# A list-scheduled fp32 encoder layer: GpSimd operations that wait for their planned VectorE predecessor on the shared SBUF path, and a planner that lets transfers land later

## The chip, the cores and the metric

One core of one Trainium2 chip. The metric is device microseconds (us) of one execution. Engine names are those of the profile: PE (TensorE matmul), PEld (its weight loads), DVE (VectorE), ACT (ScalarE), POOL (GpSimd), SP (the queue that issues every DMA here).

## The reference, cut to what matters

Two inputs, a prompt of 512 tokens and a sample of 1024, go through one encoder layer of width 1024, with the same weights:

```python
x = layer_norm(x, ln_in_g, ln_in_b)
h = x @ w_in                                   # 2048 columns: conv value, conv gate, rnn x, rnn gate
c = c_val * sigmoid(c_gate)
c = silu(layer_norm(depthwise_conv(c, width 31)))
for each of 2 directions:                      # forward, backward
    xd = depthwise_conv(r_x, width 4)
    r, i = sigmoid(xd @ w_a + b_a), sigmoid(xd @ w_x + b_x)     # 8 heads of 64
    a = exp(-8 * r * softplus(-lam)); b = sqrt(-expm1(2 log a)) * (i * xd)
    hd = linear recurrence h[t] = a[t] * h[t-1] + b[t]
rec = (hf + hb) * gelu(r_gate)
x = layer_norm(alpha * x + concat(c, rec) @ w_out)
u = depthwise_conv(x @ w_up, width 3)          # 2 x 2816 columns: val, gate
x = layer_norm(alpha * x + (gelu(gate) * val) @ w_down)
```

## The kernel before, in words

Everything is fp32. A matmul is three products of parts: every operand is split into a high part (rounded to fp32r by an ACTIVATE) and a low part (the rest, by one subtraction on DVE or POOL), and PE adds hi·hi, hi·lo and lo·hi. So each weight that is loaded has to be split by ACT, and then by DVE or POOL, before PE can use it (`split`, `weight`; some weights' low parts are written to DRAM, `lo_up_d` and `lo_down_d`, and loaded again by the later blocks).

The work comes in this order. Head: the layer norm of the input pages (128 tokens by 1024), transposes, and h of the sample and the prompt (`w_in`). Then the prompt's mixer (convolutions, gates, decay, scan), its output projection and its feed-forward part (FFN, `ffn(None)`); the sample in two blocks of 512 tokens, block 1 first: `mixer_s(1)` runs beside the prompt's FFN, `mixer_s(0)` beside `ffn(1)`, and `ffn(0)`, the last 530 us, has no mixer beside it. The FFN goes through 22 pairs of 128 columns (`up(p)`): two up projections, three taps of a convolution on ACT and DVE, gelu on ACT, one product of 128x512 on "any" of DVE and POOL (on POOL in the prompt's FFN), a split, and after some pairs the down projection, whose sums DVE adds to y. The tail is the last four pages' layer norm (`ln2`), which for two of the pages has its two 128x1024 operations (times g, plus b) on POOL, and the stores to `out_s`.

Nothing is issued in the order of this text. Each helper (`tt` L197, `stt` L206, `ts` L220, `act` L236, `dma` L247, `mm` L258, `transposes` L266) records an operation with its cost in ns, a priority, and its predecessors. `Sched.emit` (L270) then plays the list through: at each step it takes, over the five engines, the operation that could start earliest (of those ready within LOOK = 160 ns the one of the best priority), for "any" operations on the engine that would end sooner, and notes the order. The five engines' instruction streams are written out in that order, and nothing moves later. LAT holds the planned delay between engines (155 ns from DVE to POOL).

One SBUF path is modelled as shared: `takes_port` says that a POOL operation that reads SBUF, and a DVE operation with two SBUF inputs, use it one at a time, and `port` is the time from which it is free. This is in the plan alone; on the chip the two streams run as they come. A transfer's end is planned in `emit` as `bus = max(bus, t + 1500) + nbytes / 360`, so 2.96 us after its issue for 512 KB when no other is on the bus.

POOL's work is the power of -0.5 in every layer norm (128x1), the low parts of the gate inputs (128x512, `chain`: `lo_eng="pool"`), the decay product of each chain (128x512, `rg_decay(..., "pool")`), the products of the prompt's FFN, and what "any" sends there.

Of the kernel before, what the change touches and what calls it, by code (L numbers as in the profile page):

```python
# [44 lines left out]
class View:  # L45


    def __init__(self, buf, idx, post=()):
        self.buf, self.idx, self.post = buf, idx, post
        sel = buf.index[idx]  # L50
        self.n = int(sel.size)
        self.mask = buf.mask(sel)
# [73 lines left out]


class Op:
    __slots__ = ("i", "eng", "cost", "fn", "prio", "preds", "succs", "np", "rt", "end", "tab", "nbytes", "start", "both", "shared")


LAT = {("act", "dve"): 142, ("act", "pe"): 227, ("act", "pool"): 170, ("act", "act"): 143,
       ("dve", "act"): 150, ("dve", "pe"): 233, ("dve", "pool"): 155, ("dve", "dve"): 127,
       ("pe", "act"): 197, ("pe", "dve"): 196, ("pe", "pe"): 3, ("pool", "dve"): 60, ("pool", "act"): 75,
       ("pool", "pe"): 150, ("pool", "pool"): 102}
LOOK = 160
ACT_TABLE = {AF.Sigmoid: "s", AF.Tanh: "sge", AF.Gelu_apprx_tanh: "g", AF.Sqrt: "q", AF.Silu: "u", AF.Exp: "e"}


class Sched:  # L140
    def __init__(self, nc, sbuf_pool, psum_pool):
        self.nc, self.sbuf_pool, self.psum_pool = nc, sbuf_pool, psum_pool
        self.slots = {}
        self.ops = []
        self.nbuf = 0
        self.first = {}
# [77 lines left out]
    def act(self, out, a, func, scale=1.0, bias=0.0, prio=None):  # L224
        ptr = [s for s in (scale, bias) if isinstance(s, View)]
        cost = out.n / 1.2 + (51 if a.psum else 93) + 90 * len(ptr)
        f = lambda s: s() if isinstance(s, View) else s
        kw = {}
        if isinstance(scale, View) or scale != 1.0:
            kw["scale"] = None  # L230
        if isinstance(bias, View):
            kw["bias"] = None

        def emit():
            k = {n: f({"scale": scale, "bias": bias}[n]) for n in kw}
            self.nc.scalar.activation(out=out(), in_=a(), func=func, **k)  # L236
        return self.op("act", cost, emit, [a] + ptr, [out], prio, tab=ACT_TABLE.get(func))

# [13 lines left out]
    def mm(self, out, pairs, start, stop, prio=None, w=None):  # L252

        cost = len(pairs) * ((out.n / 512) * 213 + 14)

        def emit():
            for i, (a, b) in enumerate(pairs):
                self.nc.tensor.matmul(out=out(), lhsT=a(), rhs=b(), start=start and i == 0,  # L258
                                      stop=stop and i == len(pairs) - 1)
        r = [v for p in pairs for v in p]  # L260
        return self.op("pe", cost, emit, r, [out], prio)

    def transposes(self, outs_ins, whole, ident, prio=None):
        def emit():
            for o, i in outs_ins:
                self.nc.tensor.transpose(o(), i(), ident())  # L266
        return self.op("pe", 116 * len(outs_ins), emit, [i for _, i in outs_ins] + [ident], [whole], prio)


    def emit(self):  # L270
        ops = self.ops
        for o in ops:
            o.succs, o.np, o.rt, o.start = [], len(o.preds), {}, None
        for o in ops:
            for p in o.preds:
                ops[p].succs.append(o)
        engines = ("sp", "pe", "act", "dve", "pool")
        free = dict.fromkeys(engines, 0.0)
        ready = {e: [] for e in engines}
        table = "i"  # L280
        bus = 0.0

        def choices(o):
            return ("dve", "pool") if o.eng == "any" else (o.eng,)

        port = 0.0

        def takes_port(o, e):
            return e == "pool" and o.shared >= 1 or e == "dve" and o.shared >= 2

        def ready_on(o, e):
            rt = o.rt.get(e, 0.0)
            return max(rt, port) if takes_port(o, e) else rt

        def cost_on(o, e):
            return o.cost[e] if isinstance(o.cost, dict) else o.cost

        def enable(o):
            for e in choices(o):
                ready[e].append(o)  # L300
        for o in ops:
            if o.np == 0:
                enable(o)
        order = []
        while len(order) < len(ops):
            best = None
            for e in engines:
                lst = ready[e]
                if not lst:
                    continue  # L310
                t = max(free[e], min(ready_on(o, e) for o in lst))
                if best is not None and t >= best[0]:
                    continue
                pick = None
                for o in lst:
                    rt = ready_on(o, e)
                    if rt > t + LOOK:
                        continue
                    if o.eng == "any":
                        f = "pool" if e == "dve" else "dve"  # L320
                        if max(free[f], ready_on(o, f)) + o.cost[f] < max(t, rt) + o.cost[e]:
                            continue
                    key = (o.prio + (TABLE_PEN if o.tab and table not in o.tab else 0.0), o.i)
                    if pick is None or key < pick[0]:
                        pick = (key, o, max(t, rt))
                if pick is not None and (best is None or pick[2] < best[0]):
                    best = (pick[2], e, pick[1])
            t, e, o = best
            for f in choices(o):
                ready[f].remove(o)  # L330
            cost = cost_on(o, e)
            if e == "act" and o.tab and table not in o.tab:
                cost += 1283
                table = o.tab[0]
            o.eng, o.cost, o.start = e, cost, t
            free[e] = t + cost
            if takes_port(o, e):
                port = t + cost
            if e == "sp":
                bus = max(bus, t + 1500) + o.nbytes / 360.0  # L340
                o.end = bus
            else:
                o.end = t + cost
            for s in o.succs:
                for f in choices(s):
                    s.rt[f] = max(s.rt.get(f, 0.0), o.end + LAT.get((e, f), 100))
                s.np -= 1
                if s.np == 0:
                    enable(s)
            order.append(o)  # L350
        self.place()
        self.order = order
        self.makespan = max(o.end for o in ops)
        for o in order:
            if o.both:
                o.fn(o.eng)
            else:
                o.fn()


TABLE_PEN = 3.0
# [2 lines left out]
def body(ctx, tc, xp, xs, w_in, gw, w_out, w_up, w_down, par, gb, out_p, out_s):  # L364
    nc = tc.nc
    sb = ctx.enter_context(tc.tile_pool(name="sb", bufs=1))
    ps = ctx.enter_context(tc.tile_pool(name="ps", bufs=1, space=PSUM))
    S = Sched(nc, sb, ps)
    f32, f32r = F32, F32R

    x0_d = [tc.dram_tile([NP_TOK // 128, 128, D], F32, name="x0p_d"),
# [7 lines left out]

    P = S.buf("par", [NPAR])  # L380
    idn = S.buf("idn", [128])
    cst = S.buf("cst", [8])
    S.load(P.all, par, prio=1.5)

    def mk_ident():
        make_identity(nc, idn.ap())
    S.op("pool", 1500, mk_ident, [], [idn.all], prio=-1)
    S.op("pool", 100, lambda: nc.gpsimd.memset(cst[0:1](), -0.5), [], [cst[0:1]], prio=-2)
    S.op("pool", 100, lambda: nc.gpsimd.memset(cst[1:2](), 0.5), [], [cst[1:2]], prio=-2)
# [722 lines left out]
```

## Time and profile before

| what | value |
|---|---|
| time, median of 3 runs (lowest, highest) | 1616.22 us (1615.35, 1616.29) |
| the profiled execution's own time | 1616.81 us |
| its span in the profile | 1615.0 us |
| granted TensorE clock, mean of that execution | 0.993 |
| PE busy | 1556.7 us (96%), 7012 instructions |
| DVE busy | 1200.4 us (74%), 1867 instructions |
| ACT busy | 820.3 us (51%), 1019 instructions |
| POOL busy | 188.1 us (12%), 159 instructions |
| DMA queue of SP | 314.9 MB, 58.8% of 16 engines |

The span is what the profiler sees from the first to the last instruction; the execution's own time is 1.8 us more, and 0.6 us above the median of the runs. Busy time counts an instruction from its start to its end, so an instruction that is held back by something inside its run counts as busy. An engine's idle time is listed with what ended it.

### The profile page before, as it was taken

To read this page: it belongs to the slowest core of one execution; us is meant where nothing else is said; L and a number is where in the kernel's file an instruction comes from. 1 tells how busy PE (TensorE), PEld (TensorE's weight loads), DVE (VectorE), ACT (ScalarE), POOL (GpSimd) and SP (SyncE) were. 2 spreads that over 40 slices of the span, in tenths; PEclk is the share of its full clock that TensorE was granted. 3 is DMA by queue.
4 is the path that set the end of the run, shared out by engine and by line. 5 is a ranking of instruction groups with operands and counts; after the bars stand their busy time and mean duration, and the time that the engine had idled before them with its cause. 6 is when DMAs were issued, how large, how long until landed. Compare 5 with 4: busy or idle time off the path is not lost.

```text
span 1615.0 us, 19015 instructions
## 1 busy us (share of the span) xinstructions
PE 1556.7 (96%) x7012; PEld 1281.2 (79%) x7012; DVE 1200.4 (74%) x1867; ACT 820.3 (51%) x1019; POOL 188.1 (12%) x159
## 2 busy tenths in 40 slices
PE   5999999999999999999999999999999999999996
PEld 5887888887778777788888878788887888888784
DVE  8999995498989999873689899844438644545448
ACT  3737775148687974344359833352424433333341
POOL 3102121002122222010101100000001000000003
PEclk9999999999999999999999999999999999999998
DMA  9862335466567455657686676476665556555541
GB/s 359 299 219 96 126 118 187 165 208 206 158 193 223 153 189 190 202 169 248 204 259 201 214 251 202 160 253 200 195 212 196 195 194 195 202 183 195 184 162 65
DMA packets 107517, 316.09 MB, mean 196 GB/s; under 512 B 11936, under 2 KB 12064, under 8 KB 107296
## 3 DMA queue, kind: packets, MB, share of 16 engines
q1 hardware_dynamic: 107424, 314.88, 58.8%
q8 instruction: 55, 0.90, 0.2%
q14 instruction: 38, 0.31, 0.1%
HBM read 247.72 MB, written 67.11 MB: 195 GB/s over the span
## 4 chain that ended last, share of the span: by engine, by line
PE 50%; DVE 26%; ACT 10%; DMA 9%; issue 4%; SPq 0%; POOL 0%; DVEq 0%; ACTq 0%; POOLq 0%
PE b L258 48%; DVE b L206 15%; DVE b L197 9%; ACT b L236 7%; DMA b<-w_up 6%; ACT L236 3%; PE b L266 1%; DMA b<-mixs_d 1%; DMA b<-w_down 1%; DVE b L708 1%; DMA lo_in_d<-b 1%; DVE b L413 0%; DMA b<-lo_out_d 0%; DMA b<-xp 0%; SPq L247 0%
## 5 line engine op out<-in xcount | busy, mean ns | idle before, releaser
L258 PE MATMUL b<-b,b 128*128 128x512 f32 (+1 forms) x6724 | 1532.1, 389 | 24.5 <-DVE b L197 15.9
L258 PEld LDWEIGHTS b<-b,b 128*128 128x128 f32 x6724 | 1247.8, 189 | 293.6 <-DVE b L197 26.5
L206 DVE SCALAR_TENSOR_TENSOR b<-b,b,b 128x511 f32<-128x511 f32 (+12 forms) x848 | 593.0, 715 | 177.5 <-ACT b L236 156.6
L236 ACT ACTIVATE b<-b 128x1024 fp32r<-128x1024 f32 (+4 forms) x576 | 447.3, 799 | 533.6 <-PE b L258 197.2
L197 DVE TENSOR_TENSOR b<-b,b 128x512 f32<-128x512 f32 (+6 forms) x483 | 396.0, 840 | 122.8 <-ACT b L236 70.4
L236 ACT ACTIVATE b<-b,b 128x512 f32<-128x512 f32 (+1 forms) x337 | 256.9, 784 | 220.9 <-PE b L258 160.3
L197 POOL TENSOR_TENSOR b<-b,b 128x1 f32<-128x1 f32 (+3 forms) x89 | 113.6, 1282 | 674.1 <-DVE b L220 443.7
L236 ACT ACT_TABLE_LOAD x106 | 136.0, 1283 | 26.7 <-DVE b L206 23.9
L197 POOL TENSOR_TENSOR b<-b 128x512 f32<-128x512 f32 x52 | 73.3, 1409 | 609.1 <-ACT b L236 597.6
L206 DVE SCALAR_TENSOR_TENSOR b<-b,b 128x512 f32<-128x512 f32 (+2 forms) x81 | 53.6, 673 | 62.5 <-PE b L258 61.8
L413 DVE BATCH_NORM_STATS2 b<-b 128x6 f32<-128x512 f32 x84 | 56.7, 688 | 12.1 <-PE b L266 6.7
L197 DVE TENSOR_TENSOR b<-b 128x512 f32<-128x512 f32 (+3 forms) x80 | 46.5, 600 | 25.8 <-ACT b L236 24.9
L206 DVE SCALAR_TENSOR_TENSOR b<-b 128x512 f32<-128x512 f32 (+1 forms) x110 | 56.0, 518 | 6.8 <-POOL b L197 3.4
L266 PE MATMUL b<-b,b 128*128 128x128 f32 x288 | 40.0, 281 | 17.9 <-DVE b L206 12.1
L266 PEld LDWEIGHTS b<-b,b 128*128 128x128 f32 x288 | 34.8, 145 | 23.9 <-DVE b L206 10.7
L708 DVE TENSOR_TENSOR_SCAN b<-b 128x512 f32<-128x512 f32 x24 | 29.3, 1223 | 0.7
L1046 POOL MEMSET b<- 128x128 f32 x1 | 0.2, 207 | 134.6 <-PE b L258 134.6
L220 DVE TENSOR_SCALAR b<-b 128x1 f32<-128x1 f32 (+1 forms) x61 | 10.3, 171 | 1.7
L415 DVE BATCH_NORM_AGGREGATE b<-b 128x2 f32<-128x12 f32 (+1 forms) x48 | 9.5, 199 | 0.9
L243 DVE COPY b<-b 128x2 f32<-128x2 f32 x44 | 6.6, 150 | 0.0
L220 DVE TENSOR_SCALAR b<-b,b 128x512 f32<-128x512 f32 x2 | 0.9, 484 | 0.0
L900 POOL MEMSET b<- 128x1 f32 x8 | 0.3, 99 | 1.0 <-PE b L258 1.0
(11 smaller groups left out, 1.6 us busy)
## 6 DMA issues: line engine op xcount, KB each, us to landing
b<-w_up SPq DMA_DIRECT2D x132, 512.0 KB, 4.4
b<-lo_up_d SPq DMA_DIRECT2D x88, 512.0 KB, 4.2
b<-w_down SPq DMA_DIRECT2D x132, 256.0 KB, 4.0
lo_up_d<-b SPq DMA_DIRECT2D x44, 512.0 KB, 5.1
b<-lo_down_d SPq DMA_DIRECT2D x88, 256.0 KB, 3.5
b<-w_in SPq DMA_DIRECT2D x32, 512.0 KB, 5.2
b<-w_out SPq DMA_DIRECT2D x24, 512.0 KB, 4.4
lo_down_d<-b SPq DMA_DIRECT2D x44, 256.0 KB, 5.3
```

Of the source, the lines that this page charges most:

```text
L197: return self.op(eng, cost if eng == "any" else cost[eng], lambda e=eng: self.engine(e).tensor_tensor(out=out(), in0=a(), in1=b(), op=op), ...
L206: o = self.op("dve", cost, lambda: self.nc.vector.scalar_tensor_tensor(out=out(), in0=a(), scalar=s() if isinstance(s, View) else s, in1=b ...
L220: return self.op(eng, cost, lambda: e.tensor_scalar(out=out(), in0=a(), scalar1=f(s1), scalar2=f(s2), op0=op0, **({"op1": op1} if op1 is n ...
L236: self.nc.scalar.activation(out=out(), in_=a(), func=func, **k)
L243: return self.op("dve", cost, lambda: self.nc.vector.tensor_copy(out(), a()), [a], [out], prio)
L258: self.nc.tensor.matmul(out=out(), lhsT=a(), rhs=b(), start=start and i == 0, stop=stop and i == len(pairs) - 1)
L266: self.nc.tensor.transpose(o(), i(), ident())
L413: S.op("dve", c.n * 1.0417 + 69, lambda i=i, c=c: nc.vector.bn_stats(out=sm_[6 * i:6 * i + 6](), in_=c()), [c], [sm_[6 * i:6 * i + 6]], prio)
L415: S.op("dve", 211, lambda: nc.vector.bn_aggr(out=sm_[12:14](), in_=sm_[0:6 * n]().rearrange("p (a b) -> p a b", a=n)), [sm_[0:6 * n]], [sm ...
L708: S.op("dve", out.n * 2.0833 + 69, lambda: nc.vector.tensor_tensor_scan(out=out(), data0=a(), data1=b(), initial=0.0, op0=ALU.mult, op1=AL ...
L900: S.op("pool", 100, lambda z=z: nc.gpsimd.memset(z.f32(), 0.0), [], [z], ev)
L1046: S.op("pool", 200, lambda: nc.gpsimd.memset(E0.all.f32(), 0.0), [], [E0.all], 60)
```

## The change

A POOL operation that takes the shared path right after a DVE operation is planned LAT[dve, pool] = 155 ns later than the path is free, and the DVE operation, `holder`, is remembered. When the streams are written, the POOL instruction gets a dependency on that DVE instruction, so that on the chip it waits on DVE's semaphore. No DVE instruction is made to wait for POOL. Apart from that every transfer, load or store, is planned to end LAND = 1400 ns later; its wait on the chip is unchanged. Both numbers move the order of all five engines. Helpers' lines grow by 3 (`tt` is L200 after the change).

```diff
+LAND = 1400.0
...
-        port = 0.0
+        port, holder = 0.0, None
...
         def ready_on(o, e):
             rt = o.rt.get(e, 0.0)
-            return max(rt, port) if takes_port(o, e) else rt
+            if not takes_port(o, e):
+                return rt
+            return max(rt, port + (LAT["dve", "pool"] if e == "pool" and holder is not None else 0.0))
...
             if takes_port(o, e):
                 port = t + cost
+                if e == "pool":
+                    o.after = holder
+                holder = o if e == "dve" else None
             if e == "sp":
                 bus = max(bus, t + 1500) + o.nbytes / 360.0
-                o.end = bus
+                o.end = bus + LAND
...
         for o in order:
-            if o.both:
-                o.fn(o.eng)
-            else:
-                o.fn()
+            o.ins = o.fn(o.eng) if o.both else o.fn()
+            if o.after is not None:
+
+                self.tc.add_manual_dep(o.ins.ins, o.after.ins.ins.name, mybir.DependencyInfo(
+                    mybir.DependencyClass.Sync, mybir.DependencyReason.DATA), reason="port")
```

(`Sched` is given `tc` for this, and `Op` has two more slots.)

Where the order moves, at the three places that the prediction speaks of. In the rows b9, b16 are pages of the sample's input, b26 to b36 weights of `w_in` with their parts, b10 to b20 the layer norms' small values.

The head on POOL, before:

```order
L197 TENSOR_TENSOR b13_106<-b13_106,b3_116 128x1 [waits DVE_49]
L197 TENSOR_TENSOR b27_82<-b26_97,b27_82 128x1024 [waits DMAHW4_49,Activation_49]
L197 TENSOR_TENSOR b30_83<-b29_98,b30_83 128x1024 [waits DMAHW6_49,Activation_49]
L197 TENSOR_TENSOR b17_107<-b17_107,b3_116 128x1 [waits DVE_49]
L197 TENSOR_TENSOR b33_84<-b32_99,b33_84 128x1024 [waits DMAHW0_49,Activation_49]
L197 TENSOR_TENSOR b20_108<-b20_108,b3_116 128x1 [waits DVE_49]
L197 TENSOR_TENSOR b83_109<-b83_109,b3_116 128x1 [waits DVE_49]
L197 TENSOR_TENSOR b36_85<-b35_175,b36_85 128x1024 [waits DMAHW7_49,Activation_49]
```

and now:

```order
L200 TENSOR_TENSOR b13_106<-b13_106,b3_116 128x1 [waits DVE_49]
L200 TENSOR_TENSOR b27_82<-b26_97,b27_82 128x1024 [waits DMAHW4_49,Activation_49]
L200 TENSOR_TENSOR b17_107<-b17_107,b3_116 128x1 [waits DVE_49]
L200 TENSOR_TENSOR b30_83<-b29_98,b30_83 128x1024 [waits DMAHW6_49,Activation_49]
L200 TENSOR_TENSOR b20_108<-b20_108,b3_116 128x1 [waits DVE_49]
L200 TENSOR_TENSOR b33_84<-b32_99,b33_84 128x1024 [waits DMAHW0_49,Activation_49]
L200 TENSOR_TENSOR b83_109<-b83_109,b3_116 128x1 [waits DVE_49]
L200 TENSOR_TENSOR b36_85<-b35_176,b36_85 128x1024 [waits DMAHW7_49,DVE_49,Activation_49]
```

The second weight split (b30) now stands behind the power of the third page's norm (b17), whose DVE wait now names a DVE instruction behind the second STT of page 1.

The mixer of block 1 beside the prompt's FFN, on POOL (b283 is the low part of a gate input, b280 to b282 the chains' values, b324 the FFN's products), before:

```order
L197 TENSOR_TENSOR b283_2882<-b281_2885,b283_2882 128x512 [waits PE_49,Activation_49,Pool_49]
L197 TENSOR_TENSOR b283_2882<-b282_2904,b283_2882 128x512 [waits PE_49,Activation_49]
L197 TENSOR_TENSOR b280_2855<-b280_2855 128x512 [waits Activation_49]
L197 TENSOR_TENSOR b324_2914<-b324_2914 128x512 [waits Activation_49]
L197 TENSOR_TENSOR b281_2885<-b281_2885 128x512 [waits Activation_49]
```

and now:

```order
L200 TENSOR_TENSOR b283_2881<-b281_2884,b283_2881 128x512 [waits PE_49,DVE_49,Activation_49,Pool_49]
L200 TENSOR_TENSOR b283_2881<-b282_2903,b283_2881 128x512 [waits DVE_49,PE_49,Activation_49]
L200 TENSOR_TENSOR b280_2855<-b280_2855 128x512 [waits Activation_49]
L200 TENSOR_TENSOR b324_2913<-b324_2913 128x512 [waits DVE_49,Activation_49]
L200 TENSOR_TENSOR b281_2884<-b281_2884 128x512 [waits DVE_49,Activation_49]
```

The operations are the same, and four of these five now also wait for DVE. Of POOL's operations other than the powers 10 named DVE among their waits before, and 55 do now.

The tail on DVE (b686, b687 and b460 are the last pages, b739 holds g and b, b902 the last page's small values), before:

```order
L197 TENSOR_TENSOR b687_7119<-b687_7119,b893_11629 128x512 [waits PE_49]
L197 TENSOR_TENSOR b686_8111<-b686_8111,b739_7884 128x1024 [waits Activation_49]
L413 BN_STATS b902_11643<-b687_7119 128x6 [waits DVE_49]
L415 BN_AGGR b902_11643<-b902_11643 128x2 [waits DVE_49]
L220 TENSOR_SCALAR b902_11643<-b902_11643 128x1 [waits DVE_49]
L197 TENSOR_TENSOR b686_8111<-b686_8111,b739_7884 128x1024
L197 TENSOR_TENSOR b687_7119<-b687_7119,b739_7884 128x1024 [waits Activation_49]
L197 TENSOR_TENSOR b687_7119<-b687_7119,b739_7884 128x1024 [waits DVE_49]
L206 SCALAR_TENSOR_TENSOR b687_7119<-b687_7119,b902_11643,b739_7884 128x1024
L206 SCALAR_TENSOR_TENSOR b687_7119<-b687_7119,b902_11643,b739_7884 128x1024 [waits DVE_49,Pool_49]
```

and now:

```order
L200 TENSOR_TENSOR b687_7035<-b687_7035,b893_11629 128x512 [waits PE_49]
L200 TENSOR_TENSOR b686_8111<-b686_8111,b739_7864 128x1024 [waits Activation_49]
L200 TENSOR_TENSOR b686_8111<-b686_8111,b739_7864 128x1024 [waits DVE_49]
L200 TENSOR_TENSOR b687_7035<-b687_7035,b739_7864 128x1024 [waits Activation_49]
L200 TENSOR_TENSOR b687_7035<-b687_7035,b739_7864 128x1024 [waits DVE_49]
L422 BN_STATS b902_11643<-b687_7035 128x6
L424 BN_AGGR b902_11643<-b902_11643 128x2 [waits DVE_49]
L223 TENSOR_SCALAR b902_11643<-b902_11643 128x1 [waits DVE_49]
L209 SCALAR_TENSOR_TENSOR b687_7035<-b687_7035,b902_11643,b739_7864 128x1024
L209 SCALAR_TENSOR_TENSOR b687_7035<-b687_7035,b902_11643,b739_7864 128x1024 [waits Pool_49]
```

The last page's statistics now come behind the four 128x1024 operations of the two pages before it. On POOL the first operation on b460 now waits for the last of these four (before: for ACT alone), and the last power (b902) waits for the first of the two SCALAR_TENSOR_TENSOR (before: for the TENSOR_SCALAR).

Engine choices move too: the 128x512 product of the last FFN is on POOL once (six times before), two more low parts and one norm operation of 128x1024 go to DVE, and two 128x1024 and one 128x511 go to POOL. ACT loads its tables 98 times (106 before). Matmuls and DMAs are the same in number.

## Rows read from the trace of the kernel before

**Rows 1.** Busy time by stage: head, prompt's mixer, two mixer stages, last FFN.

```profile
core 0: us, PE busy (x) PEld busy (x) DVE busy (x) ACT busy (x) POOL busy (x), PEclk, DMA share, GB/s
0.00:50.00 50.00, 32.50 (x239) 31.17 (x240) 43.24 (x64) 21.07 (x26) 16.46 (x20) 1.00 0.95 352
50.00:330.00 280.00, 277.99 (x1271) 229.66 (x1270) 233.69 (x355) 162.61 (x204) 38.20 (x30) 1.00 0.50 170
330.00:750.00 420.00, 405.36 (x1770) 328.69 (x1769) 371.84 (x499) 275.76 (x339) 76.20 (x53) 0.99 0.60 193
750.00:1060.00 310.00, 306.03 (x1370) 252.17 (x1369) 260.41 (x421) 158.75 (x191) 26.46 (x30) 1.00 0.65 215
1060.00:1590.00 530.00, 525.69 (x2331) 432.31 (x2330) 272.08 (x500) 197.35 (x256) 17.03 (x18) 1.00 0.57 189
```

**Rows 2.** Waits of PE, 0 to 50 us: total us, times, longest.

```profile
PE b L266 <- DVE b L206: 11.6, 2, 10.7
PE b L266 <- DVE b L415: 5.7, 1, 5.7
```

**Rows 3.** Timeline of the head, DVE and PE: start, length, idle before.

```profile
15.15 3.13 DVE L206 SCALAR_TENSOR_TENSOR b<-b,b,b 128x1024 f32<-128x1024 f32 x1
25.72 2.75 DVE L206 SCALAR_TENSOR_TENSOR b<-b,b,b 128x1024 f32<-128x1024 f32 x1
18.43 1.94 PE L266 MATMUL b<-b,b 128*128 128x128 f32 x8 [5.75 <-DVE b L415]
```

**Rows 4.** Waits of PE, 330 to 750 us.

```profile
PE b L258 <- DVE b L197: 8.1, 10, 3.4
PE b L258 <- POOL b L197: 1.4, 1, 1.4
```

**Rows 5.** Timeline, PE behind its waits at 450 and 602 us.

```profile
449.92 5.36 PE L258 MATMUL b<-b,b 128*128 128x512 f32 x16 [1.37 <-POOL b L197]
601.88 6.44 PE L258 MATMUL b<-b,b 128*128 128x512 f32 x20 [3.42 <-DVE b L197]
```

**Rows 6.** Busy time of the stretch behind the first, and of a quiet one.

```profile
449.90:453.30 3.40, 3.38 (x9) 2.67 (x9) 3.26 (x7) 3.34 (x5) 1.22 (x1) 0.54 0.69 248
1070.00:1200.00 130.00, 130.00 (x576) 107.69 (x575) 47.73 (x80) 44.97 (x54) 0.31 (x2) 1.00 0.63 206
```

**Rows 7.** Groups by form, POOL then ACT: busy us, mean ns | idle before.

```profile
L197 POOL TENSOR_TENSOR b<-b,b 128x512 fp32r<-128x512 f32 x24 | 36.2, 1511 | 176.5 <-ACT b L236 161.0 <-PE b L258 15.0 <-POOL b L197 0.4
L236 ACT ACT_TABLE_LOAD x106 | 136.0, 1283 | 26.7 <-DVE b L206 23.9
```

**Rows 8.** Waits of ACT, whole span; and the page's DMA issues (KB, us to landing).

```profile
ACT b L236 <- DMA b<-w_up: 99.5, 43, 5.7
...
b<-w_up SPq DMA_DIRECT2D x132, 512.0 KB, 4.4
```

**Rows 9.** Waits of PE, 1060 to 1590 us.

```profile
PE b L258 <- DVE b L197: 2.1, 6, 0.5
PE b L258 <- DMA b<-lo_down_d: 1.7, 2, 1.1
```

**Rows 10.** Timeline at 1357 us, a pair of the last FFN.

```profile
1356.85 1.29 POOL L197 TENSOR_TENSOR b<-b 128x512 f32<-128x512 f32 x1 [48.38 <-ACT b L236]
1356.90 1.26 DVE L197 TENSOR_TENSOR b<-b 128x1 f32<-128x1 f32 x1 [0.72 <-ACT b L236]
1358.81 0.50 PE L258 MATMUL b<-b,b 128*128 128x512 f32 x1 [0.41 <-DVE b L197]
```

**Rows 11.** Timeline of the tail.

```profile
1599.19 1.82 DVE L197 TENSOR_TENSOR b<-b,b 128x512 f32<-128x512 f32 x2 [0.81 <-PE b L258]
1600.50 7.13 POOL L197 TENSOR_TENSOR b<-b,b 128x1024 f32<-128x1024 f32 x3 [2.31 <-ACT b L236]
1601.97 6.75 DVE L197 TENSOR_TENSOR b<-b,b 128x1024 f32<-128x1024 f32 x3
1608.64 2.67 DVE L206 SCALAR_TENSOR_TENSOR b<-b,b,b 128x1024 f32<-128x1024 f32 x2
```

More of the change, by code (lines that the diff above doesn't have):

```diff
@@ L128 @@
 class Op:
-    __slots__ = ("i", "eng", "cost", "fn", "prio", "preds", "succs", "np", "rt", "end", "tab", "nbytes", "start", "both", "shared")
+    __slots__ = ("i", "eng", "cost", "fn", "prio", "preds", "succs", "np", "rt", "end", "tab", "nbytes", "start", "both", "shared", "after", "ins")
 LAT = {("act", "dve"): 142, ("act", "pe"): 227, ("act", "pool"): 170, ("act", "act"): 143,
@@ L136, with __init__ @@
 LOOK = 160
+LAND = 1400.0
 ACT_TABLE = {AF.Sigmoid: "s", AF.Tanh: "sge", AF.Gelu_apprx_tanh: "g", AF.Sqrt: "q", AF.Silu: "u", AF.Exp: "e"}
 class Sched:
-    def __init__(self, nc, sbuf_pool, psum_pool):
+    def __init__(self, tc, sbuf_pool, psum_pool):
+        nc = tc.nc
+        self.tc = tc
         self.nc, self.sbuf_pool, self.psum_pool = nc, sbuf_pool, psum_pool
@@ L272, in emit @@
         for o in ops:
-            o.succs, o.np, o.rt, o.start = [], len(o.preds), {}, None
+            o.succs, o.np, o.rt, o.start, o.after = [], len(o.preds), {}, None, None
         for o in ops:
@@ L367, in body @@
     ps = ctx.enter_context(tc.tile_pool(name="ps", bufs=1, space=PSUM))
-    S = Sched(nc, sb, ps)
+    S = Sched(tc, sb, ps)
     f32, f32r = F32, F32R
```

## The prediction

> **What bounds the kernel.** I began with the time of each engine by stage [rows 1]. PE is busy in nearly all of each stage but the head: it idles 17.5 us before 50 us (50.00 less 32.50), 2.0 in the prompt's mixer, 14.6 and 4.0 in the two stages with a mixer beside an FFN, 4.3 in the last FFN. The steady price of a 128x512 matmul is 130 us / 576 = 0.226 us [rows 6], and the change leaves the matmuls as they are; so it can win only in these 42 us, in the tail, and where PE's clock is low. [...]
>
> Then I read what PE waited for. In the head nearly all is DVE [rows 2]. In 330 to 750 us most is DVE again, and one wait is POOL itself [rows 4]. In the last FFN it is 2.1 us of DVE and 1.7 of a reloaded weight [rows 9].
>
> Last I looked at how POOL and DVE hold each other up. At 15.15 us a SCALAR_TENSOR_TENSOR of 128x1024 took 3.13 us, at 25.72 one took 2.75 [rows 3]; two undisturbed ones at the end took 2.67 together, 1.33 each [rows 11]. In both places POOL was working. At 1356.90 a DVE operation on 128x1 took 1.26 us while POOL's product ran from 1356.85 for 1.29 [rows 10]. The lock costs POOL too: its 24 low parts took 1511 ns in the mean [rows 7], against 1.29 for that product.
>
> **The change, part by part.** Five terms, all against the profiled execution.
>
> *Head: −2.0 us (0 to −3.2).* The first blocked SCALAR_TENSOR_TENSOR is what page 1's transposes come from, and PE stood for 5.75 us until they began at 18.43 [rows 3]. In the new POOL order the second weight split stands behind a power that now waits for DVE to be past it, so the 3.13 becomes about 1.33: 1.8 us. The second, at 25.72, gives 1.4 more by the same sum. Both together are the lower end. But the DMA share in the head is 0.95 [rows 1], so some of what PE wins there it will spend waiting for pages and weights: this is why I take about two thirds, and zero as the other end.
>
> *Prompt's mixer, 50 to 330 us: −1.5 (0 to −2.0).* The whole idle time is 2.0 us [rows 1], so that is the end; the low part of the gate weights moves from POOL to DVE here, and with it POOL's blocking of DVE goes.
>
> *The two mixer stages, 330 to 1060 us: −3.5 (−22.8 to +10).* 18.6 us of idle time [rows 1] and three slow-clock stretches at some 1.4 us each are the most there is: 22.8. Here lies most of the change: POOL's operations beside the powers that name DVE in their waits go from 10 to 55. What the order gives back I can tie to rows at one place, the wait for POOL [rows 4] at 449.92 [rows 5] with its slow stretch, 2.7 us. For the rest I take 0.8. The largest wait, 3.42 us at 601.88, names DVE [rows 5], and DVE is busy 372 of 420 us in this stage [rows 1], so I do not count on it. LAND has a row of its own: ACT, which issues in order, stood 99.5 us behind 43 loads of `w_up` [rows 8]; they landed 4.4 us after issue in the median, where the plan had 2.96 and now has 4.36. A plan that knows this puts other work ahead of the split; that is why the far end stays whole. The other end is four new events like that at 449.92, about +10. The eight table loads that go are 8 × 1.283 = 10.3 us of ACT [rows 7], but ACT has over 140 us idle in the first of these stages [rows 1], and I cost them at nothing; if ACT bound a stretch of it, some of the 10.3 would come as a gain, and this lies inside the range. The 128x1024 operations that change engine here are two onto DVE and two onto POOL: nothing.
>
> *Last FFN: −1.5 (0 to −2.1).* Six pairs have their product on POOL; now one. On DVE it costs some 0.6 us, the half of the pair in the tail that has this size [rows 11], and DVE is busy 272 of 530 us [rows 1], so it is covered; in return the 1.26 us block goes, and with it PE's wait of 0.41 behind DVE's next operations [rows 10]. All six waits for DVE sum to 2.1 [rows 9]; five of the six would give 1.75, and I take 1.5, since the product now stands in DVE's own stream. The order at the wait for the reloaded weight is the same in both kernels, so its 1.7 us stays.
>
> *Tail: +1.5 (+1.0 to +2.8).* The pair of DVE operations at 1599.19 (one of 128x512, one of 128x1024 that ran beside no operation of POOL for most of its length) took 1.82 us, some 0.6 and 1.2 [rows 11]. The three 128x1024 operations behind it took 6.75 us instead of 3 × 1.2, with POOL's between. Now four run unblocked from 1599.8 to about 1604.7, because POOL's first one waits for the last of them. Then come the last page's statistics; before they lay between the first two rows of DVE, from 1601.01 to 1601.97, so 1.0 us, to 1605.7. But POOL started at 1604.8; at 2.4 us unblocked (7.13 / 3 [rows 11], which is a mean with a power in it, and so a rough estimate) it holds the path to 1607.2, and the first SCALAR_TENSOR_TENSOR, which stands behind it, ends at about 1608.4. The power waits for that one: 1609.0. Now POOL's last 128x1024 operation and DVE's last one want the path together, 2.4 + 1.3, whichever is first: 1612.8, where DVE before ended at 1608.64 + 2.67 = 1611.31. That is +1.5; the tail wins its blocked time and loses more, since now the statistics, the first of the two and the power stand in a row behind all four.
>
> Sum: −2.0 −1.5 −3.5 −1.5 +1.5 = **−7.0 us**. The profiled execution's 1616.81 becomes 1609.8; the median of the runs lies 0.59 below that execution, which gives 1609.2. I say 1609.0.
>
> [...] The trace shows DVE operations following each other without a gap (three in 6.75 us), so the one behind the named predecessor begins before POOL hears of it [rows 11]. [...]
>
> **Rivals.**
> *Slower (0.18).* POOL's operation now begins one DVE operation late or more, and where it is the low part of a gate input, the gate matmul waits; PE issues in order, so it idles, and its clock falls as at 449.92. The price is that event's, 1.37 + 1.35 = 2.7 us [rows 5, 6]. Sixteen of the 24 low parts [rows 7] lie in the two mixer stages, and in the new order 11 of them wait for DVE, none before. Behind a waiting POOL operation stand the decay products and the prompt's products, too. The other four terms give −3.5, so it decides from three net new events on: 3 × 2.7 − 3.5 = +4.6, or 1620.8. For it: DVE is 372 of 420 busy, so the predecessor is often late. Against it: POOL has most of its time free (76 of 420 busy), and the low parts have some lead.
>
> *No change (0.20).* The freed DVE time was hidden, the head is held by its transfers, and the middle stage wins one thing and loses another: −1.5 (prompt) −1.5 (last FFN) +1.5 (tail) = −1.5, or 1614.7. For it: PE's busy share, and that most of DVE's blocked time lies beside a busy PE. That the change does not do what it says belongs here, with little weight, since the order shows the waits.
>
> *Much faster (0.15).* The plan now has transfers and the path about as they are, and two thirds of the 22.8 us in the mixer stages go: −15 −3.5 = −18.5, or 1597.7. For it: the 99.5 us of ACT behind loads [rows 8]. Against: most of PE's waits there name DVE, which has little time left.
>
> **How the numbers follow.** The forecast itself has 0.47. The range from 1598.0 to 1621.0 reaches to both outer cases, whose far halves are left out; the summed bounds (1587 to 1629) would need every term at its end at once. A measurement here can tell 0.2%, 3.2 us, from no change: faster is below 1613.0, slower above 1619.5. Faster gets the forecast and the much faster case, 0.62; same 0.20; slower 0.18.
>
> **What would show it.** Right: the two long SCALAR_TENSOR_TENSOR of the head at about 1.3 us, transposes before 17 us; POOL's low parts longer in idle before them, with DVE as releaser, and DVE's blocked ones few; PE's waits for DVE in 1060 to 1590 below 1 us; DVE's last operation ending some 12.9 us after its last sum from PE is added, against 11.4 before (1599.8 to 1611.3). Wrong: PE's waits for POOL in 330 to 750 at several us, with a granted clock of about 0.5 behind them (the slower rival), or PE's idle time there below 5 us (the much faster one).

## The result and the profile after

The changed kernel takes 1588.24 us (median of 4 runs, 1587.26 to 1588.92) against 1616.12 for before: a ratio of 0.9823, 95% interval 0.9808 to 0.9838. The forecast was 1609.0 in a range from 1598.0 to 1621.0; the gain of 28 us is four times the forecast one and lies outside the range. The direction was right, and the rival "much faster" (1597.7) was the case that happened, though it too stopped 9.5 us short.

Busy time of each engine by stage in the profile of after, with the bounds of the last two stages moved with the work:

```profile
core 0: us, PE busy (x) PEld busy (x) DVE busy (x) ACT busy (x) POOL busy (x), PEclk, DMA share, GB/s
0.00:50.00 50.00, 34.87 (x254) 33.37 (x255) 43.22 (x69) 22.96 (x29) 14.57 (x20) 1.00 0.98 383
50.00:330.00 280.00, 279.84 (x1281) 231.95 (x1281) 232.61 (x361) 161.25 (x204) 31.93 (x30) 1.00 0.50 165
330.00:750.00 420.00, 416.06 (x1841) 341.45 (x1840) 369.69 (x500) 270.75 (x336) 66.23 (x52) 1.00 0.63 205
750.00:1040.00 290.00, 288.94 (x1298) 238.76 (x1298) 255.02 (x418) 156.64 (x190) 25.81 (x32) 1.00 0.67 219
1040.00:1550.00 510.00, 507.66 (x2259) 419.57 (x2258) 257.63 (x482) 190.91 (x248) 7.85 (x11) 1.00 0.59 193
```

Against [rows 1], PE's idle time in 330 to 750 us falls from 14.6 to 3.9 us, and PE does 71 more matmuls in that window. Its waits there, which were led by 8.1 us behind DVE [rows 4], are now:

```profile
PE b L261 <- DMA b<-lo_out_d: 2.0, 1, 2.0
PE b L261 <- DVE b L200: 1.2, 3, 0.5
PE b L261 <- DVE b L209: 0.6, 1, 0.6
```

To give each stage its share I compare when the n-th matmul starts, since PE's 7012 matmuls are the same in number in both kernels (their order differs in places, so the n-th is not always the same one). The 250th starts 2.6 us earlier than before, the 1500th (about the end of the prompt's mixer) 5.1, the 4600th (about the end of the second mixer stage) 25.9, the last 29.9; the span is 28.7 us shorter. So the head gives −2.6, the prompt −2.5, the mixer stages −20.8, the last FFN −4.0, and the tail +1.1, each rounded.

PE's busy time falls too, from 1556.7 to 1546.6 us, for as many matmuls. A part of that is the clock. Before, the mixer stages held three stretches of 3.4 us at a granted clock of 0.50, the one at 450 us [rows 6] and two more, from 603.2 and from 668.1 us; now they hold one, from 724.4 us, behind the longest wait that is left, the 2.0 us for `lo_out_d`. Two windows of before, then one of after (PEclk, the third number from the end, is a mean over the window):

```profile
601.90:606.90 5.00, 5.00 (x15) 3.99 (x16) 4.87 (x8) 4.96 (x7) 1.29 (x1) 0.66 0.45 114
667.90:671.50 3.60, 3.60 (x10) 2.82 (x9) 3.53 (x6) 0.63 (x1) 0.29 (x1) 0.53 0.89 288
722.00:729.00 7.00, 5.42 (x17) 4.29 (x18) 0.69 (x1) 0.98 (x2) 0.00 (x0) 0.76 0.79 316
```

At the prediction's price, 1.35 us a stretch (nine matmuls took 3.38 us [rows 6], and nine at the steady 0.226 are 2.03), the two that went are some 2.7 of the 10.1 us, which is an estimate. The clock is not all: from the 4600th matmul to the last no stretch was slow in either kernel, and PE's busy time there fell by 2.0 us. So some of the time that PE loses lies inside the busy time that the profile gives its matmuls.

DVE no longer holds POOL up. POOL's groups by form (busy us, mean ns | idle before and what ended it):

```profile
L200 POOL TENSOR_TENSOR b<-b 128x512 f32<-128x512 f32 x47 | 60.7, 1293 | 332.3 <-ACT b L239 141.6 <-DVE b L200 101.5 <-DVE b L209 76.1
L200 POOL TENSOR_TENSOR b<-b,b 128x512 fp32r<-128x512 f32 x24 | 30.9, 1295 | 159.7 <-ACT b L239 64.3 <-DVE b L209 50.8 <-DVE b L200 38.8
L200 POOL TENSOR_TENSOR b<-b,b 128x1 f32<-128x1 f32 x48 | 26.3, 549 | 733.2 <-DVE b L223 581.6 <-DVE b L209 144.0 <-DVE b L200 7.4
```

The 24 low parts take 1295 ns in the mean where they took 1511 [rows 7], none of the 71 operations of 128x512 takes more than 1304, and part of what ends POOL's idle time is now DVE. POOL still holds DVE up, in fewer places: of DVE's operations beside one of POOL, 25 took over 0.3 us more than the median of their kind before (29.6 us in sum), and 9 do now (7.7 us). One place shows how it goes; the timeline of after at 356 us, POOL beside DVE:

```profile
355.40 1.22 DVE L200 TENSOR_TENSOR b<-b,b 128x1024 fp32r<-128x1024 f32 x1
356.53 2.97 DVE L209 SCALAR_TENSOR_TENSOR b<-b,b,b 128x504 f32<-128x504 f32 x4
356.76 1.29 POOL L200 TENSOR_TENSOR b<-b,b 128x512 fp32r<-128x512 f32 x1 [29.39 <-DVE b L200]
```

The DVE split that POOL is made to wait for ends at 356.62, and POOL starts at 356.76. DVE's next operation has started already, but it and the one behind it add a convolution's taps up in PSUM, with one SBUF input each, and by the plan's `takes_port` need no shared path: 2.97 us for four is 0.74 each, about the 0.75 of their kind in before, and POOL's 1.29 is undisturbed too. That is what the plan meant by putting POOL there.

The head answers to [rows 3]; DVE, then PE:

```profile
15.57 1.23 DVE L209 SCALAR_TENSOR_TENSOR b<-b,b,b 128x1024 f32<-128x1024 f32 x1
16.72 0.15 DVE L223 TENSOR_SCALAR b<-b 128x1 f32<-128x1 f32 x1
...
16.95 1.94 PE L269 MATMUL b<-b,b 128*128 128x128 f32 x8 [4.09 <-DVE b L209]
```

The operation that took 3.13 us takes 1.23, and page 1's transposes start at 16.95 instead of 18.43. The tail answers to [rows 11]:

```profile
1569.29 5.48 DVE L200 TENSOR_TENSOR b<-b,b 128x512 f32<-128x512 f32 x5 [0.81 <-PE b L261]
1574.92 2.34 POOL L200 TENSOR_TENSOR b<-b,b 128x1024 f32<-128x1024 f32 x1 [6.63 <-DVE b L200]
1575.72 2.61 DVE L209 SCALAR_TENSOR_TENSOR b<-b,b,b 128x1024 f32<-128x1024 f32 x1
1578.42 2.85 POOL L200 TENSOR_TENSOR b<-b,b 128x1 f32<-128x1 f32 x2 [1.16 <-DVE b L209]
1579.00 3.35 DVE L209 SCALAR_TENSOR_TENSOR b<-b,b,b 128x1024 f32<-128x1024 f32 x1 [0.66 <-POOL b L200]
```

The five operations, one of 128x512 and four of 128x1024, now take 5.48 us without a block; then each of the last two SCALAR_TENSOR_TENSOR stands behind one of POOL's 128x1024 operations (2.61 and 3.35 us), and DVE ends 12.4 us after the last sum was added (1570.0 to 1582.35), where it was 11.4.

### The profile page after: what moved, and what is told of

It is laid out like the page before. It is cut to its first block, busy times and chain, and to the rows that moved or that the text cites. A ratio compares the mean times of both kernels' runs of the same rounds, so it can differ in the third digit from the quotient of the medians.

```text
span 1586.3 us, 19021 instructions
## 1 busy us (share of the span) xinstructions
PE 1546.6 (98%) x7012; PEld 1280.7 (81%) x7012; DVE 1187.1 (75%) x1872; ACT 809.0 (51%) x1011; POOL 158.4 (10%) x154
## 4 chain that ended last, share of the span: by engine, by line
PE 79%; DVE 12%; ACT 5%; DMA 2%; issue 2%; POOL 0%; SPq 0%; POOLq 0%; DVEq 0%; ACTq 0%
PE b L261 77%; DVE b L209 7%; DVE b L200 5%; ACT b L239 3%; PE b L269 2%; ACT L239 1%; DMA b<-w_up 1%; DMA b<-lo_out_d 0%; DMA b<-xp 0%; DVE b L717 0%; DMA b<-lo_down_d 0%; POOL b L200 0%; DVE b L422 0%; SPq L250 0%; DVE b L223 0%
## 5 line engine op out<-in xcount | busy, mean ns | idle before, releaser
L200 DVE TENSOR_TENSOR b<-b,b 128x512 f32<-128x512 f32 (+4 forms) x484 | 389.9, 825 | 112.9 <-ACT b L239 63.7
L200 POOL TENSOR_TENSOR b<-b,b 128x1 f32<-128x1 f32 (+3 forms) x88 | 95.2, 1088 | 945.8 <-DVE b L223 581.6
L239 ACT ACT_TABLE_LOAD x98 | 125.7, 1283 | 21.2 <-DVE b L209 17.9
L200 POOL TENSOR_TENSOR b<-b 128x512 f32<-128x512 f32 (+1 forms) x48 | 62.0, 1293 | 340.2 <-ACT b L239 141.6
L200 DVE TENSOR_TENSOR b<-b 128x1 f32<-128x1 f32 (+3 forms) x84 | 42.9, 527 | 22.5 <-ACT b L239 21.2
```

Source lines behind the costliest of these rows:

```text
L200: return self.op(eng, cost if eng == "any" else cost[eng], lambda e=eng: self.engine(e).tensor_tensor(out=out(), in0=a(), in1=b(), op=op), ...
```

## The experiments

All kernels are edits of the changed one, and each is compared with runs of before on its own chip (medians of before from 1615.5 to 1618.9, so the ratio and the stages say more than the time; where the text gives what a kernel wins, it is against before on its chip). "Front" is the start of the 1500th matmul, "mixers" the time from there to the 4600th, "last" from there to the last matmul, "tail" the rest of the span, all in us of the one profiled execution, which for g3, f3 and f4 was 2.4 to 3.9 us faster than the kernel's median. "155" is the planned delay of POOL behind DVE, and "port part" below is that delay and the waits together.

| kernel | LAND | 155 | waits | time | ratio [95%] | front | mixers | last | tail |
|---|---|---|---|---|---|---|---|---|---|
| before | 0 | no | no | 1616.12 | | 328.7 | 722.2 | 547.8 | 16.3 |
| the change | 1400 | yes | yes | 1588.24 | 0.9823 [0.9808, 0.9838] | 323.6 | 701.4 | 543.8 | 17.4 |
| e1 | 0 | no | yes | 1598.56 | 0.9899 [0.9880, 0.9919] | 324.6 | 710.3 | 543.7 | 16.9 |
| e2 | 1400 | yes | no | 1603.75 | 0.9928 [0.9913, 0.9944] | 329.1 | 711.5 | 543.6 | 17.9 |
| e3 | 1400 | no | no | 1594.65 | 0.9877 [0.9862, 0.9892] | 328.9 | 699.2 | 547.7 | 16.3 |
| e4 | 0 | yes | yes | 1596.02 | 0.9887 [0.9870, 0.9905] | 323.5 | 709.2 | 544.2 | 17.4 |
| e5 | 1400 | no | yes | 1588.15 | 0.9823 [0.9808, 0.9838] | 324.6 | 697.4 | 545.9 | 16.9 |
| e6 | 1300 | yes | yes | 1592.88 | 0.9852 [0.9837, 0.9866] | 323.3 | 706.4 | 543.8 | 17.4 |
| e7 | 1500 | yes | yes | 1600.60 | 0.9899 [0.9884, 0.9914] | 323.9 | 709.8 | 547.5 | 17.4 |
| e8 | 2800 | yes | yes | 1598.30 | 0.9887 [0.9871, 0.9904] | 324.6 | 705.6 | 548.6 | 17.4 |
| f1 | 100 | no | no | 1610.46 | 0.9953 [0.9938, 0.9967] | 329.0 | 715.0 | 547.9 | 16.3 |
| f2 | 1300 | no | no | 1591.20 | 0.9833 [0.9819, 0.9848] | 328.9 | 700.3 | 544.2 | 16.3 |
| f3 | 1500 | no | no | 1599.13 | 0.9888 [0.9871, 0.9904] | 328.8 | 701.9 | 547.6 | 16.3 |
| f4 | 100 | yes | yes | 1607.21 | 0.9930 [0.9915, 0.9945] | 324.2 | 715.9 | 545.5 | 17.4 |
| g1 | 1300 | no | yes | 1584.25 | 0.9812 [0.9797, 0.9826] | 324.1 | 697.2 | 544.1 | 16.9 |
| g2 | 1500 | no | yes | 1586.99 | 0.9825 [0.9811, 0.9840] | 324.8 | 696.1 | 547.3 | 16.9 |
| g3 | w_up | no | no | 1607.79 | 0.9956 [0.9939, 0.9973] | 328.7 | 712.6 | 544.5 | 16.3 |
| h1 | w_up, w_down | no | no | 1606.47 | 0.9932 [0.9917, 0.9947] | 328.9 | 714.6 | 543.8 | 16.3 |
| h2 | all loads | no | no | 1598.69 | 0.9889 [0.9872, 0.9906] | 332.1 | 700.2 | 547.9 | 16.3 |
| i1 | w_up, w_down, mixer's loads | no | no | 1593.03 | 0.9843 [0.9826, 0.9859] | 328.8 | 701.6 | 544.2 | 16.3 |

(In the last four rows LAND is 1400 for the transfers named and 0 for others.)

**Taking the change apart.** The three edits, alone or together, and LAND set to another number:

```diff
-LAND = 1400.0
+LAND = 0.0
...
-            return max(rt, port + (LAT["dve", "pool"] if e == "pool" and holder is not None else 0.0))
+            return max(rt, port)
...
-            if o.after is not None:
+            if False and o.after is not None:
```

e1 has the first two (the waits alone; every engine's order is that of before), e2 the third (the order of the change, instruction for instruction), e3 the last two, e4 the first.

e1: 

> The order of before, with the real waits alone: no 155 ns in the plan and LAND at 0. Theory A (the real waits win the time, since POOL then works beside the DVE operations that the plan put beside it): 1600 us or less, DVE blocked by POOL in under 12 of 25 places. Theory B (the order that LAND gives wins the time): 1612 to 1617. Theory C (both are needed, since only a plan that holds on the chip is worth ordering by): 1605 to 1613.

e2: 

> The order of the change, instruction for instruction, without the real waits. Theory A: 1606 us or more, close to before. Theory B: 1588 to 1592. Theory C: 1595 to 1606, with long POOL and DVE operations back as in the kernel before.

e3: 

> LAND alone: no wait, no 155 ns in the plan. Theory A: 1612 to 1617 us, as before. Theory B: 1592 or less. Theory C: 1598 to 1608.

e4: 

> The port part alone: the waits and the 155 ns in the plan, LAND at 0. Theory A: 1592 us or less. Theory B: 1611 to 1617. Theory C: 1598 to 1610.

e1 and e2 are the clean pair, since each shares its order with another kernel. The change wins 27.9 us, e1 16.9, e2 11.7 and e3 20.8. So the waits are worth 16.9 us on the order of before, and on that of the change 16.2 (27.9 less 11.7, across two chips). Theory B (the order alone) falls with that. But the order alone is worth 11.7 us (e2), and LAND alone 20.8 (e3), so theory A falls as well. Theory C, that neither is worth much without the other, falls too: the waits alone and LAND alone each win more than half of the whole, and together (e5, below) they win less than their sum. e4's 1596.02 lies between what A and C said of it.

The mean length of POOL's operations follows the waits: for the two groups of 128x512 it is 1293 to 1296 ns in the change, e1, e5 and g1, with the waits, and 1409 to 1511 in before, e2, e3, h1 and i1, without. The groups of e1, then of e2, then of e3:

```profile
L200 POOL TENSOR_TENSOR b<-b 128x512 f32<-128x512 f32 x52 | 67.3, 1295 | 597.8 <-DVE b L200 292.4 <-ACT b L239 166.5 <-DVE b L209 102.7
```

```profile
L200 POOL TENSOR_TENSOR b<-b 128x512 f32<-128x512 f32 x47 | 67.2, 1432 | 328.1 <-ACT b L239 287.4 <-DVE b L209 23.0 <-issue 10.2
```

```profile
L200 POOL TENSOR_TENSOR b<-b 128x512 f32<-128x512 f32 x52 | 75.0, 1444 | 585.4 <-ACT b L239 578.5 <-DMA b<-w_up 6.9
```

Theory A's other sign, DVE blocked in under 12 of 25 places in e1, did not come: by the count above it is 15 (11.8 us). In e2 it is 28 and in e3 22, so what their orders win is not won by less blocking. e3, with POOL and DVE blocking each other nearly as before, has hardly a PE wait left in 330 to 750 us:

```profile
PE b L261 <- ACT b L239: 0.9, 1, 0.9
PE b L261 <- DVE b L200: 0.8, 3, 0.3
PE b L261 <- POOL b L200: 0.3, 1, 0.3
```

**Is it the value of LAND, or luck of the order?**

e5: 

> LAND and the real waits, without the 155 ns in the plan. If the two parts add where they lie in different stages (LAND 23 us in the mixer stages, the waits 2.5 in the head, 1.6 in the prompt and 4.2 in the last FFN): 1583 to 1587 us, under the change. If the plan needs the 155 ns to hold on the chip: 1590 to 1597.

e6: 

> The change with LAND at 1300. Theory P (a landing time near the true one is what counts): 1586 to 1591 us. Theory L (each order is one draw among many, and 1400 was a good one): more than 4 us away from the change, most likely 1592 to 1600.

e7: 

> The change with LAND at 1500. Theory P: 1586 to 1591 us. Theory L: 1592 to 1600.

e8: 

> The change with LAND at 2800, so loads of 512 KB planned at 5.8 us where 4.4 is measured. Theory P: 1592 us or more, since work is now put behind loads that have long landed. A theory that late is always safe: 1586 to 1591. Theory L: anywhere from 1586 to 1600.

With the whole port part, theory L came nearer: 1300 and 1500 stand 5 and 12 us from the change. e8 fits both; its mixer stages are shorter than those of 1300 and 1500. e5 gave 1588.15, just above the 1583 to 1587 that adding the parts gives; its mixer stages were the best so far, and the last FFN 2 us worse. So I set LAND low and high without the port part, and low with it.

f1: 

> LAND at 100 and no port part: a plan that knows as little of the loads as before, in a somewhat different order. Theory P (what LAND wins is that loads are planned near their true landing): 1612 to 1618 us. Theory L (the mixer stages' time is a draw of the order, and before was a poor one): 1594 to 1610.

f2: 

> LAND at 1300 alone, no port part. Theory P: 1592 to 1597 us, as with 1400 alone (1594.65). Theory L: anywhere from 1592 to 1616, more than 3 us from 1594.65. The waits being worth 15 to 17 us on one and the same order, 1592.88 with the port part would make it some 1609.

f3: 

> LAND at 1500 alone, no port part. Theory P: 1592 to 1597 us. Theory L: anywhere from 1592 to 1618; some 1616 if the waits are worth the same 15 to 17 us here (1600.60 with the port part).

f4: 

> LAND at 100 with the whole port part. Theory P: 1594 to 1599 us, as with LAND at 0 (1596.02). Theory L: 1586 to 1602, more than 3 us from 1596. By both the head, the prompt and the last FFN keep their 8 us, so under 1608.

By the total the answer is mixed: f1's 1610.46 lies between what the theories said, f2's 1591.20 just below both, f4's 1607.21 above both, and f3's 1599.13 above theory P, with a last FFN like that of before. In the mixer stages without the port part it is plain. LAND of 0 and 100 gives 722.2 and 715.0 us, 1300, 1400 and 1500 give 700.3, 699.2 and 701.9. There theory P holds, as far as it was tried: no kernel without the port part plans later than 1500, so that landing near the true time is what counts, and not only landing late enough, is not shown. With the whole port part the picture is gone: 709.2 and 715.9 at 0 and 100, 706.4, 701.4, 709.8 and 705.6 at 1300, 1400, 1500 and 2800.

f2 and f3 also miss the 1609 and 1616 that I worked out from a fixed worth of the waits: the whole port part is worth −7.1 us at 1400 and +2.1 and +1.9 at 1300 and 1500, where the intervals overlap. What it wins in the front (5 us) it gives back in the mixer stages at 1300 and 1500.

**The 155 ns.**

g1: 

> LAND at 1300 and the real waits, without the 155 ns in the plan. If planning the 155 ns is what costs time in the mixer stages (PE's matmuls 1500 to 4600 took 706.4 us with it, 700.3 without port part): mixer stages 696 to 701, and 1583 to 1588 us in all. If it is a draw of the order: mixer stages anywhere from 697 to 710, and 1584 to 1598.

g2: 

> The same with LAND at 1500 (709.8 us with the 155 ns, 701.9 without port part). If the 155 ns cost time: mixer stages 697 to 703, and 1585 to 1592 in all. If it is a draw: mixer stages 697 to 712, and 1585 to 1601.

With LAND at 1400, 1300 and 1500 the 155 ns in the plan cost time in the mixer stages: with the waits, but without the 155 ns, these take 697.4, 697.2 and 696.1 us, with both 701.4, 706.4 and 709.8. Without waits it is the same way round (e3 against e2: 699.2 and 711.5). It is not so with LAND at 0 (e1 710.3, e4 709.2), and at 1400 the whole kernel is no slower for them (1588.24 against 1588.15), since the front and the last FFN give most of it back. Why an honest delay makes these orders worse was not tried further. g1 is the fastest kernel of the study at 1584.25 us, and on its own chip 1.9% under before; its interval overlaps that of the change, so that it beats the change is likely, not shown. PE's window from 330 to 750 us in g1, nearly without idle time:

```profile
330.00:750.00 420.00, 418.11 (x1861) 344.29 (x1860) 368.27 (x500) 273.51 (x339) 66.11 (x52) 1.00 0.63 208
```

**Which transfers.** My reading was that LAND wins by ACT's waits for the loads of `w_up` [rows 8], which fell from 99.5 to 41.5 us over the whole span in e3. g3, h1, h2 and i1 give LAND to some transfers alone:

```diff
-                o.end = bus + LAND
+                o.end = bus + o.land
...
-            S.load(v, src_tile(kind, m)[:, cols], prio)
+            ld = S.load(v, src_tile(kind, m)[:, cols], prio)
+            if kind == "up":
+                ld.land = LAND
```

(h1: `if kind in ("up", "down")`; h2: in the helper `load`, for every load through it; i1: as h1, and for the mixer's loads of `mixs_d` and `hf_d`.)

g3: 

> LAND at 1400 for the loads of w_up alone, no port part. If what LAND wins is that ACT no longer stands in order behind splits whose loads have not landed: ACT's waits for w_up 35 to 55 us in sum (99.5 before, 41.5 with LAND for all), mixer stages 697 to 706 us, 1592 to 1600 in all. If the stores and reloads matter as much: mixer stages 708 to 718, and 1602 to 1612.

h1: 

> LAND at 1400 for the loads of w_up and w_down, no port part. If ACT's waits for both weights are what LAND wins by (33.1 us for w_down before, 36.1 with LAND on w_up alone, 14.1 with LAND for all): mixer stages 697 to 703 us, 1592 to 1598 in all. If the reloads or the stores matter too: mixer stages 704 to 714, 1599 to 1610.

h2: 

> LAND at 1400 for all loads of weights, pages and reloads, none for stores, no port part. If only loads matter: mixer stages 697 to 703 us, 1592 to 1598 in all, as with LAND for all (699.2 and 1594.65). If the end of stores matters, since reloads wait for it: mixer stages 704 to 714, 1599 to 1610.

i1: 

> LAND at 1400 for w_up, w_down and the mixer's own loads (mixs_d, hf_d), none for other loads and stores, no port part. If the mixer's loads, planned too early, are what the middle stages lose by: mixer stages 697 to 705 us, 1592 to 1602 in all. If they are not (the rest is reloaded low parts, w_in, w_out and pages): mixer stages 708 to 718, 1602 to 1612.

The reading falls. h2 says that the stores don't matter there (its mixer stages take 700.2 us; it loses 3 us in the front). ACT's waits for `w_up` over the whole span are about the same in g3 and in h2 (in this order below), and g3's lie where I had expected them:

```profile
ACT b L240 <- DMA b<-w_up: 53.9, 28, 4.6
```

```profile
ACT b L240 <- DMA b<-w_up: 54.5, 26, 9.3
```

and yet g3's mixer stages take 712.6 us and h2's 700.2. In h1 ACT's waits for `w_down` are down as in e3 (14.1), those for `w_up` about two thirds of the way:

```profile
ACT b L240 <- DMA b<-w_up: 61.7, 28, 9.0
...
ACT b L240 <- DMA b<-w_down: 15.6, 11, 4.1
```

and its mixer stages take 714.6 us, no better than g3 and f1. With the mixer's own loads added, i1 takes 701.6. PE's waits in 330 to 750 us, of h1 and then of i1:

```profile
PE b L262 <- DVE b L201: 13.4, 11, 2.7
```

```profile
PE b L262 <- DVE b L201: 2.0, 4, 1.1
PE b L262 <- ACT b L240: 0.9, 1, 0.9
PE b L262 <- DMA b<-lo_out_d: 0.8, 1, 0.8
PE b L262 <- POOL b L201: 0.3, 1, 0.3
```

Of the nine kernels without any port part, the five that plan the mixer's loads 1300 ns or more later take 699.2 to 701.9 us there, the four that don't 712.6 to 722.2. All five plan the loads of `w_up` and `w_down` later as well; the mixer's loads alone were not tried. The engines hardly wait for these loads themselves (about 2 us for `mixs_d` in that window in before and in i1), so I take it that what changes is where the plan puts the work behind them among DVE's other work. By which step PE then waits less for DVE stays open.

## Why the prediction was right or wrong

*The failed step is the mixer stages' term:* "−3.5 (−22.8 to +10)", and in it "DVE is busy 372 of 420 us in this stage [rows 1], so I do not count on it". It measured −20.8, of which 13.6 are PE's idle time (18.6 before, 5.0 now); the rest lies in its busy time, some 2.7 of it in the slow stretches. DVE is as busy as before (369.7 of 420 us), and PE's waits for it went all the same; since LAND alone, which moves operations and adds no wait, takes them away too (e3), what PE waited for was the place of a DVE operation in the queue, not DVE's load. The term's far end counts three slow stretches at some 1.4 us each: the trace of before has the three, 3.4 us at 0.50 each, and the 1.4 is the estimate from [rows 6]. The term also put LAND itself at nothing and left it to the far end. By e1 the waits alone take 11.9 us off these stages, by e3 LAND alone 23.0. I had seen that LAND might do it, as the much faster rival with 0.15, and gave the wrong reason (ACT's 99.5 us). The sign that I had named for that rival, less than 5 us of PE idle time in 330 to 750 us, came (3.9); of the signs for the forecast one did not: POOL's idle time before its low parts is not longer (159.7 us against 176.5 [rows 7]).

*The range* cut that rival in half. The summed lower ends (1587) were set aside since "every term at its end at once" seemed unlikely; that is nearly what happened. It was not one cause: LAND alone wins in the mixer stages and nowhere else (e3), the waits alone win in the front and the last FFN too (e1).

*The bounds counted too little.* PE's idle time was taken as all there is to win in the prompt, and only its waits for DVE in the last FFN. The prompt gave 2.5 where I capped it at 2.0, the last FFN 4.0 where the cap was 2.1; there idle time fell by 2.0 and busy time by as much.

*Head (−2.0; −2.6 measured)* was right, and the waits and the new order each do it by themselves: at the 250th matmul e1, with the old order, is 2.5 us ahead of before, e2, with the new order and no waits, 2.0. LAND alone does not (e3 is 0.2 behind). *Prompt (−1.5; −2.5)* needs the waits: e2 has lost all its lead by the 1500th matmul (329.1 against 328.7), e1 has 4.1.

*Last FFN (−1.5; −4.0)* moved the right way, but its mechanism is not what the runs show. PE's waits for DVE's sums there are 0.3 us now against 2.1 [rows 9], and the stage takes 543.6 with the product moved (e2) and 543.7 with the waits on the old order (e1). But f2, which has six products on POOL, no waits, and DVE still blocked beside the product (1.26 us at 1333.90, as in [rows 10]), takes 544.2 and has the same 0.3 us. So the block was not what had to go; another order does it as well, and which of these acts in the change is open.

*Tail (+1.5; +1.1)* was right; e1 and e3 put 0.6 of it on the waits and nothing on LAND, so the rest comes with the 155 ns.

*The slower rival* did not happen. It has POOL begin one DVE operation late or more, held up by what DVE runs behind the named predecessor. POOL still holds DVE up: in the tail POOL starts at 1574.92, and the SCALAR_TENSOR_TENSOR that starts at 1575.72 ends 1.07 us after POOL does, at 1578.33. At 356 us DVE's next operation does start before POOL (356.53 against 356.76). But the plan takes that one to be off the path, and POOL, which starts 0.14 us after its predecessor's end there, takes 1.29 us. What DVE ran beside each of POOL's other operations is not shown; that none of the 71 took more than 1304 ns suggests that no DVE operation held them up. That a DVE operation on the path, started first, would hold POOL up behind its wait was my estimate; no run shows it. I had priced the wait without looking at what stands behind the named predecessor on DVE.

## What to carry to other kernels

Where an order is planned on paper, holding one engine's stream to the plan by a semaphore can win without any other edit (here 16 to 17 us on an unchanged order); look at what stands behind the predecessor before pricing the wait. A planner's landing time is worth measuring and putting in (here 13 to 23 us in the mixer stages where the 155 ns were left out, hardly anything at 1300 and 1500 where they were not); but every such number moves the whole order, so try neighbours of it (here 1588, 1593 and 1601 us for 1400, 1300 and 1500) before calling one of them the effect. And a stage's idle time on the bounding engine is not a cap on what can be won there (here 20.8 us where 18.6 were idle).

## What the runs showed of the hardware

With a wait on DVE's instruction POOL's 128x512 operations took 1293 to 1296 ns in the mean (the change, e1, e5, g1), without it 1409 to 1511 (before, e2, e3, h1): the blocking cost POOL 0.1 to 0.2 us in the mean. A DVE operation that the plan takes to be off the path ran beside POOL with neither lengthened (0.74 us each and 1.29, at 356 us); on the path POOL still held DVE up (2.61 and 3.35 us against 1.23, in the tail). POOL started 0.14 us after its predecessor ended (356.62 to 356.76), near the 155 ns that the plan assumes; putting those 155 ns into the plan made the mixer stages longer nevertheless, in the orders with LAND at 1300 to 1500. PE's granted clock was 0.50 for 3.4 us beside or behind some of its waits, three times in the mixer stages before (from 449.6 us, at a wait of 1.37 that ended at 449.9; from 603.2, after one of 3.42 that ended at 601.9; from 668.1, after one of 0.53 that ended at 667.1) and once now (from 724.4, after one of 2.00 that ended at 723.6).
